# Conditioning vectors of a two-layer trunk: two empty steps between the last sum and the finishing products

## The chip, the cores and the metric

The kernel runs on one core of a Trainium2 chip. The metric is the device time of one execution in microseconds (us); of several executions the median is given. A profile is one execution, recorded by the hardware profiler; its span runs from the first to the last instruction. The engines are TensorE (PE, with its weight loads as PEld), VectorE (DVE), ScalarE (ACT), GpSimd (POOL) and SyncE (SP), whose queue issues nearly all transfers.

## The reference, cut to what matters

256 tokens of width 2048 go through two layers. Each layer has a token mixer (forgetting attention in layer 0, sliding-window attention in layer 1) and a gated feed-forward part with a short convolution. All is float32. What the change touches is the conditioning:

```python
c_act = jax.nn.silu(c)
for i in range(DEPTH):
    mod = c_act @ ada_w[i] + ada_b[i]
    sh1, sc1, g1, sh2, sc2, g2 = jnp.split(mod[:, None, :], 6, axis=-1)
    h = x * (1.0 + sc1) + sh1
    y = mixer(h)
    x = layer_norm(DEEPNORM_ALPHA * x + (1.0 + g1) * y, ...)
    h = x * (1.0 + sc2) + sh2
    y = conv_ffn(h, ...)
    x = layer_norm(DEEPNORM_ALPHA * x + (1.0 + g2) * y, ...)
```

Per layer six vectors of 2048 numbers are needed: shift and scale before the mixer (numbers 0 and 1), the gate behind it (2), and the same three for the feed-forward part (3, 4, 5). Each is a product of one row of 2048 with a 2048x2048 matrix, 16 MB that is read once.

## The kernel before, in words

Weights stream through SBUF in tiles of 128x1024 (512 KB). Every weight tile is split into a high part (`wh`, an ACT cast, L285) and a low part (`wl`, a DVE subtraction, L296), and PE multiplies both; one weight tile is twelve PE instructions of up to 512 columns in most stages. The function that PE runs for one weight tile, `go` in `stream`, ends with `tick`. The program thus advances tile by tile, and all side work is cut into steps that `tick` hands out.

Two of the twelve conditioning vectors are made in the opening; the other ten are made by the generator `ada_vector`, one after the other, in the order of `ada_list`: (0,2), (0,3), (0,4), (0,5), (1,0), (1,1), (1,3), (1,2), (1,4), (1,5), each a pair of layer and number. One vector is 32 sums: for each of 16 blocks of 128 rows, and for each half of the 2048 columns, a tile `wa` of the matrix (512 KB) is loaded by SP's queue (L434), and one DVE instruction adds it, scaled by a number per partition, to the accumulator `acc` (L438 for the first block, L440 for the others). What then stands in `acc` still has to be summed over its 128 partitions. That is done by finishing products on PE with a matrix of ones (`sm`): for a shift or a scale 16 products of one column each, four to a step; for a gate four products of 512 columns, one to a step. A last DVE instruction (`cv`, L463, or the gate's, L454) adds the bias.

How many steps `ada_vector` gets is set by a rate per weight tile, a number of the stage:

```python
    def ada_tick():
        ada["debt"] += ada["rate"]
        while ada["debt"] >= 1.0:
            ada["debt"] -= 1.0
            ada_step()
```

With the last step, which ends the vector, one vector takes 32 + 4 + 1 = 37 steps. The rate is 1.0 to 1.7 in layer 0's mixer, 0.52 and 0.8 in its feed-forward part, 0.3 at the very start of layer 1's mixer, then 0.95 and 0.9, and 0.4 in the last feed-forward part. When number 4 of a layer is done, the generator holds until the next boundary has been passed.

At a boundary between a mixer and a feed-forward part (or between layers) `between` calls `ada_need` for the shift and the scale that it needs. If one isn't done, `ada_need` hands out steps on the spot until it is. `modulate` follows: PE runs ten 512-column products (`warm`) that compute nothing that is used, transposes the first token block of `x`, runs six more, transposes the second block, and starts on the next weights, while DVE and ACT finish the normalisation.

The framework's scheduler puts the instructions on each engine in an order of its own, but those passed to `pin` with its second argument true keep the program's order among each other: the sums, the column products, `cv`, the residual of the last column block (L662 to L672) and the normalisation (L691) are among them. The loads are not. All `w`, `wa` and `ln` tiles share one pool of ten buffers that are taken in turn.

Of the kernel before, what the change touches and what calls it, by code (L numbers as in the profile page):

```python
# [41 lines left out]
def hybrid_trunk(ctx: ExitStack, tc: tile.TileContext, a: dict, out: bass.AP):  # L42
# [14 lines left out]
    def wtile(name="w"):  # L57
        return wp.tile([P, 2, WB], F32, tag="w", name=name)
# [7 lines left out]
    def bank(name="sm"):  # L66
        return psp.tile([P, 512], F32, tag="ps", name=name)
# [7 lines left out]
    def mm(o, lhsT, rhs, start=False, stop=False, **kw):  # L75
        return nc.tensor.matmul(o, lhsT, rhs, start=start, stop=stop, **kw)  # L76

    def pin(ins, on=True):

        if on:  # L80
            tc.keep_in_program_order(ins)
# [344 lines left out]
    def ada_vector(l, v):  # L426
        row = v % 3 == 2
        acc = cst.tile([P, D], F32, tag="acc", name="acc")
        part = lambda c, n: acc[:, c:c + n]
        step_ = D // 2  # L430
        for k in range(KC):
            for c in range(0, D, D // 2):
                w = wtile("wa").rearrange("p a f -> p (a f)")
                pin(nc.sync.dma_start(w, a["ada_w"][l, k * P:(k + 1) * P, v * D + c:v * D + c + D // 2]), False)  # L434
                for o in range(0, D // 2, step_):
                    ac, wo = part(c + o, step_), w[:, o:o + step_]
                    if k == 0:
                        pin(nc.vector.tensor_scalar_mul(ac, wo, cact[:, 0:1]), True)  # L438
                    else:
                        pin(nc.vector.scalar_tensor_tensor(ac, wo, cact[:, k:k + 1], ac,  # L440
                                                           op0=ALU.mult, op1=ALU.add), True)
                yield
        if row:
            while not ada["gate_free"]:
                yield
            ada["gate_free"] = False
            g = cst.tile([P, D], F32, tag="gate", name="gate")
            nc.gpsimd.dma_start(g, a["ada_b"][l, v * D:(v + 1) * D].partition_broadcast(P))
            for j in range(D // 512):
                ps = bank()  # L450
                mm(ps, ones, acc[:, j * 512:(j + 1) * 512], start=True, stop=True)
                yield
                gj = g[:, j * 512:(j + 1) * 512]
                nc.vector.scalar_tensor_tensor(gj, ps, 1.0, gj, op0=ALU.add, op1=ALU.add)  # L454
            gates[l, v] = g
            return
        ps = bank()
        for k in range(KC):
            pin(mm(ps[:, k:k + 1], part(k * P, P), ones[:, 0:1], start=True, stop=True))
            if k % 4 == 3:  # L460
                yield
        cv = cst.tile([P, KC], F32, tag=f"cv{v}", name="cv")
        pin(nc.vector.scalar_tensor_tensor(cv, ps[:, :KC], 1.0 if v % 3 else 0.0,  # L463
                                           acol[:, l, v * KC:(v + 1) * KC], op0=ALU.add, op1=ALU.add), True)
        cols[l, v] = cv
        if v == 4:
            ada["held"] = True

    def ada_step():
        if ada["gen"] is None:  # L470
            if not ada_list or ada.get("held"):
                return
            ada["gen"] = ada_vector(*ada_list.pop(0))
        if next(ada["gen"], ada) is ada:
            ada["gen"] = None
# [720 lines left out]
    for t in range(NT):  # L1196
        mu, rs, _ = moments[t]
# [34 lines left out]
```

## Time and profile before

| | |
|---|---|
| time, median of 3 runs | 2243.58 us (2242.21 to 2245.87) |
| the profiled execution: its time | 2244.19 us |
| its span | 2242.4 us |
| busy in the span: PE, DVE, ACT | 2201.2, 1854.7, 1193.0 us |
| moved by transfers | 602.68 MB |

The boundary before layer 0's feed-forward part shows in the trace at 461.75 us (the start of the ten warm products), the one before layer 1's mixer at 1213.75, and the one before layer 1's feed-forward part at 1491. Busy time of PE counts a product from its start to a modelled end, so that PE can be called busy while products come slower than they could; the idle time ahead of an instruction and the start times are the better guide.

### The profile page before, as it was taken

Reading aid. Unit: us, or ns where it says so; the run is one execution under the profiler, and the core shown is the slowest. Engines: PE = TensorE matmul, PEld = TensorE weight load, DVE = VectorE, ACT = ScalarE, POOL = GpSimd, SP = SyncE. Lnnn points to the kernel's source line nnn. Section 1 sums busy time; section 2 is a strip of 40 time slices with the busy share of each in tenths; the row PEclk is TensorE's granted clock in tenths of the full one; section 3 lists DMA queues with packets and bytes.
Section 4 is the critical chain, followed back from the end, with each engine's and each line's share of the span. In section 5 each row is a group of like instructions: output and inputs, shape, how many; then the busy total and the mean of one; then the engine's idle time right before and its main releaser. Section 6 shows DMA issues by size and latency. Waiting matters only on the chain.

```text
span 2242.4 us, 33367 instructions
## 1 busy us (share of the span) xinstructions
PE 2201.2 (98%) x12206; PEld 1890.4 (84%) x12206; DVE 1854.7 (83%) x2689; ACT 1193.0 (53%) x1873; POOL 20.0 (1%) x51
## 2 busy tenths in 40 slices
PE   7999999999999999999999999999999999999997
PEld 6999898788888888888888788888888888888886
DVE  7989998989988968978978989889988655676766
ACT  4546554455656433655534578646655533555542
POOL 0001000000000000000000000000000000000000
PEclk9999999999999999999999999999999999999999
DMA  9999999969878889878887867778887556666553
GB/s 359 390 358 336 358 364 334 336 217 313 304 240 282 320 290 330 284 230 282 281 307 281 283 194 266 235 248 291 284 270 239 185 195 190 189 190 193 189 196 114
DMA packets 287429, 602.68 MB, mean 269 GB/s; under 512 B 21846, under 2 KB 55576, under 8 KB 286752
## 3 DMA queue, kind: packets, MB, share of 16 engines
q1 hardware_dynamic: 286208, 595.86, 78.2%
q0 software_dynamic: 1056, 4.69, 0.7%
q8 instruction: 95, 1.56, 0.3%
q14 instruction: 70, 0.57, 0.1%
HBM read 598.37 MB, written 2.10 MB: 268 GB/s over the span
## 4 chain that ended last, share of the span: by engine, by line
PE 88%; DVE 7%; ACT 2%; issue 1%; DMA 1%; SPq 0%; DVEq 0%; ACTq 0%
PE wd L76 43%; PE xs L76 33%; PE ws L76 6%; DVE wl L296 2%; DVE acc L440 2%; PE sm L76 1%; PE S L76 1%; PE o L76 1%; ACT wh L285 1%; PE warm L76 1%; PE T L762 0%; DMA wo<-in_ada_w_dram 0%; DVE pr L738 0%; PE cps L76 0%; DVE oacc L590 0%
## 5 line engine op out<-in xcount | busy, mean ns | idle before, releaser
L285 ACT CAST wh<-w 128x1024 fp32r<-128x1024 f32 x728 | 764.3, 1051 | 775.9 <-PE wd L76 283.3
L296 DVE TENSOR_TENSOR wl<-w,wh 128x1024 fp32r<-128x1024 f32 x728 | 888.1, 1222 | 302.2 <-ACT wh L285 285.0
L76 PE MATMUL wd<-hHL,wh 128*128 128x512 f32 (+1 forms) x2832 | 718.2, 395 | 0.2
L76 PEld LDWEIGHTS wd<-hHL,wh 128*128 128x128 f32 x2832 | 504.6, 188 | 98.5 <-issue 2.9
L76 PEld LDWEIGHTS wd<-hHL,wl 128*128 128x128 f32 x2816 | 373.4, 188 | 31.0
L440 DVE SCALAR_TENSOR_TENSOR acc<-wa,cact,acc 128x1024 f32<-128x1024 f32 x300 | 380.9, 1279 | 0.1
L76 PE MATMUL wd<-hHL,wl 128*128 128x256 f32 x2816 | 380.0, 277 | 0.0
L76 PE MATMUL xs<-wh,gT 128*128 128x512 f32 x1408 | 350.0, 390 | 0.0
L76 PEld LDWEIGHTS xs<-wh,gT 128*128 128x128 f32 x1408 | 263.4, 188 | 54.2
L76 PE MATMUL xs<-wl,gT 128*128 128x512 f32 x704 | 189.6, 389 | 0.0
L76 PE MATMUL xs<-wh,hHL 128*128 128x512 f32 x704 | 185.5, 401 | 1.8 <-ACT wh L285 1.4
L76 PEld LDWEIGHTS xs<-wl,gT 128*128 128x128 f32 x704 | 132.1, 188 | 27.6
L76 PEld LDWEIGHTS xs<-wh,hHL 128*128 128x128 f32 x704 | 128.7, 190 | 28.6 <-ACT wh L285 1.6
L1119 ACT ACTIVATE u<-s,ccol 128x256 f32<-128x256 f32 x176 | 104.7, 599 | 68.3 <-DVE s L1114 49.6
L76 PE MATMUL ws<-hHL,wh 128*128 128x256 f32 x1024 | 132.6, 282 | 4.8 <-ACT wh L285 2.4
L76 PEld LDWEIGHTS ws<-hHL,wh 128*128 128x128 f32 x1024 | 124.8, 189 | 8.5 <-ACT wh L285 4.4
L76 PE MATMUL xs<-wh,oT 128*128 128x512 f32 x384 | 99.6, 397 | 1.7 <-ACT wh L285 1.6
L76 PE MATMUL xs<-wl,hHL 128*128 128x512 f32 x352 | 96.8, 395 | 0.8 <-DVE wl L296 0.6
L1120 DVE SCALAR_TENSOR_TENSOR u<-s,ccol,u 128x255 f32<-128x255 f32 x176 | 84.1, 479 | 5.7 <-ACT u L1119 5.7
L590 DVE SCALAR_TENSOR_TENSOR oacc<-wo,cact,oacc 128x512 f32<-128x512 f32 x111 | 79.5, 747 | 9.2 <-DMA wo<-in_ada_w_dram 5.3
L1122 DVE SCALAR_TENSOR_TENSOR u<-s,ccol,u 128x254 f32<-128x254 f32 x176 | 84.0, 478 | 1.1
L76 PEld LDWEIGHTS xs<-wh,oT 128*128 128x128 f32 x384 | 69.5, 188 | 16.6 <-ACT wh L285 2.8
(223 smaller groups left out, 1639.8 us busy)
## 6 DMA issues: line engine op xcount, KB each, us to landing
w<-in_ffn_w_up_dram SPq DMA_DIRECT2D x352, 512.0 KB, 4.6
wa<-in_ada_w_dram SPq DMA_DIRECT2D x320, 512.0 KB, 5.2
w<-in_ffn_w_down_dram SPq DMA_DIRECT2D x176, 512.0 KB, 4.3
w<-in_fox_w_in_dram SPq DMA_DIRECT2D x96, 512.0 KB, 6.6
wo<-in_ada_w_dram SPq DMA_DIRECT2D x128, 256.0 KB, 6.7
w<-in_swa_w_in_dram SPq DMA_DIRECT2D x40, 512.0 KB, 4.9
w<-in_fox_w_o_dram SPq DMA_DIRECT2D x32, 512.0 KB, 5.5
w<-in_swa_w_o_dram SPq DMA_DIRECT2D x32, 512.0 KB, 5.5
```

Source lines behind the costliest of these rows:

```text
L76: return nc.tensor.matmul(o, lhsT, rhs, start=start, stop=stop, **kw)
L285: pin(nc.scalar.copy(h, w), False)
L296: pin(nc.vector.tensor_tensor(l, w, f32(h), op=ALU.subtract), go in behind or tied[0] > 0)
L440: pin(nc.vector.scalar_tensor_tensor(ac, wo, cact[:, k:k + 1], ac, op0=ALU.mult, op1=ALU.add), True)
L590: nc.vector.scalar_tensor_tensor(ac, wk, cact[:, kc:kc + 1], ac, op0=ALU.mult, op1=ALU.add)
L1119: nc.scalar.activation(u, s, AF.Identity, bias=cw(CW, f), scale=cw(2, f))
L1120: nc.vector.scalar_tensor_tensor(u[:, 1:], s[:, :S - 1], cw(1, f), u[:, 1:], op0=ALU.mult, op1=ALU.add)
L1122: nc.vector.scalar_tensor_tensor(u[:, 2:], s[:, :S - 2], cw(0, f), u[:, 2:], op0=ALU.mult, op1=ALU.add)
```

## The change

Behind the last sum of a vector the generator now gives back the step twice without doing anything. Each vector so takes 39 steps in place of 37, and its finishing products are written two steps further down in the program. The rates, the products and the sums are the same.

```diff
@@ -440,6 +440,8 @@
                         pin(nc.vector.scalar_tensor_tensor(ac, wo, cact[:, k:k + 1], ac,
                                                            op0=ALU.mult, op1=ALU.add), True)
                 yield
+        for _ in range(2):
+            yield
         if row:
             while not ada["gate_free"]:
                 yield
```

Ten vectors times two steps make 20 steps, and each vector begins later than the one ahead of it by two more. Lines behind L442 have numbers that are higher by two in the changed kernel.

The first place is PE's order at the first vector, the gate (0,2), in layer 0's mixer. `sm<-acc,ones` is a finishing product, `ws` and `xs` are products of weight tiles, `T` is a transposition in the attention. Before:

```order
L76 MATMUL ws<-hHL,wh 128x256 x16
L76 MATMUL ws<-hHL,wl 128x256 x8
L76 MATMUL sm<-acc,ones 128x512
L762 MATMUL T<-ident,pr 128x128 x3
L76 MATMUL xs<-wh,hHL 128x512 x8
L76 MATMUL xs<-wl,hHL 128x512 x4
L76 MATMUL sm<-acc,ones 128x512 x2
```

and now:

```order
L76 MATMUL ws<-hHL,wh 128x256 x16
L76 MATMUL ws<-hHL,wl 128x256 x8
L764 MATMUL T<-ident,pr 128x128 x3
L76 MATMUL xs<-wh,hHL 128x512 x8
L76 MATMUL xs<-wl,hHL 128x512 x4
L76 MATMUL sm<-acc,ones 128x512
```

The first finishing product has moved behind one weight tile (eight and four products) and one set of transpositions.

The second place is PE's order at the boundary before layer 1's feed-forward part. Before, the 16 products of (1,4) stood in groups of four between the weight tiles of the output projection, the last group three weight tiles ahead of its end; the end itself read:

```order
L76 MATMUL xs<-wh,hHL 128x512 x4
L76 MATMUL xs<-wl,hHL 128x512 x2
L76 MATMUL warm<-ones 128x512 x10
L545 MATMUL sm<-ident,x 128x128 x4
L76 MATMUL warm<-ones 128x512 x6
L545 MATMUL sm<-ident,x 128x128 x4
```

Now:

```order
L76 MATMUL xs<-wh,hHL 128x512 x4
L76 MATMUL xs<-wl,hHL 128x512 x2
L76 MATMUL sm<-ones,acc 128x1 x16
L76 MATMUL warm<-ones 128x512 x10
L547 MATMUL sm<-ident,x 128x128 x4
L76 MATMUL warm<-ones 128x512 x6
L547 MATMUL sm<-ident,x 128x128 x4
```

All 16 products stand between the projection's last product and the first warm one: the vector isn't done when `between` asks for it, and `ada_need` hands out its last 11 steps there.

The third place is DVE's order at the same boundary, from the statistics of the second token block on. Before:

```order
L668 BN_AGGR mv<-stats 128x2
L670 TENSOR_SCALAR rs<-mv 128x1
L691 TENSOR_SCALAR x<-x,mv,rs 128x256 x2
L513 TENSOR_SCALAR t<-sm,G,B 128x256 x2
L516 TENSOR_TENSOR hHL<-t,hHL 128x256 x2
```

Now:

```order
L670 BN_AGGR mv<-stats 128x2
L672 TENSOR_SCALAR rs<-mv 128x1
L440 SCALAR_TENSOR_TENSOR acc<-wa,cact,acc 128x1024 x4
L465 SCALAR_TENSOR_TENSOR cv<-sm,acol 128x16
L725 TENSOR_TENSOR G<-cv,lcol 128x16
L726 TENSOR_TENSOR B<-cv,lcol 128x16
L727 TENSOR_TENSOR B<-B,cv 128x16
L693 TENSOR_SCALAR x<-x,mv,rs 128x256 x2
```

The last four sums, `cv` and the three instructions that use it now stand between the statistics and the normalisation; before, `cv` and the three stood ahead of the last residual. Six more sums of the vector now stand between the start of the third column block's residual and the last residual, where there was none.

## The prediction

> **What bounds the kernel now.** First the page's busy times, then the waits of PE alone, then the chain of waits.
>
> ```profile
> PE 2201.2 (98%) x12206; PEld 1890.4 (84%) x12206; DVE 1854.7 (83%) x2689; ACT 1193.0 (53%) x1873; POOL 20.0 (1%) x51
> PE 88%; DVE 7%; ACT 2%; issue 1%; DMA 1%; SPq 0%; DVEq 0%; ACTq 0%
> PE sm L76 <- DVE acc L440: 3.5, 2, 3.0
> PE xs L76 <- ACT wh L285: 3.0, 4, 1.4
> ```
>
> PE is the bound: it is idle for 2242.4 - 2201.2 = 41 us in all. So an edit that leaves PE's products alone can win only what PE waits for, and it loses whatever it puts ahead of PE's queue. In the third row finishing products (`sm`) wait for sums (L440) twice, 3.5 us together, 3.0 of them in one piece. That is the wait at which two steps' delay can be aimed. It is the first vector, (0,2):
>
> ```profile
> 254.79 1.10 PE L76 MATMUL ws<-hHL,wl 128*128 128x256 f32 x8
> 258.92 1.12 PE L76 MATMUL sm<-acc,ones 128*128 128x512 f32 x2 [3.02 <-DVE acc L440]
> 260.25 3.55 PE L76 MATMUL xs<-wh,hHL 128*128 128x512 f32 x8
> 257.58 2.48 DVE L440 SCALAR_TENSOR_TENSOR acc<-wa,cact,acc 128x1024 f32<-128x1024 f32 x2
> 256.00:259.00 3.00, 0.09 (x1) 0.09 (x1) 2.94 (x6) 3.00 (x9) 0.00 (x0) 1.00 1.01 387
> 259.00:262.00 3.00, 3.00 (x9) 2.18 (x10) 3.00 (x8) 2.74 (x7) 0.00 (x0) 0.67 1.06 408
> 262.00:264.00 2.00, 2.00 (x7) 1.52 (x7) 2.00 (x5) 1.71 (x5) 0.00 (x0) 0.65 1.04 388
> 264.00:266.00 2.00, 2.00 (x8) 1.15 (x7) 2.00 (x6) 2.00 (x7) 0.00 (x0) 1.00 0.99 367
> ```
>
> The last four rows are stretches of time with the busy time of each engine; the third number from the end is the granted PE clock. PE sits still for 3.02 us and then gets 0.67 and 0.65 of its clock for 5 us, which costs 3 x 0.33 + 2 x 0.35 = 1.7 us more. The stall is worth 4.7 us.
>
> **Part 1: the stall at (0,2) goes, -4.5.** In PE's new order a set of transpositions and one `xs` weight tile come ahead of the first product. A tile takes 2.75 us (from row to row below: 336.78 to 339.53), so with the transpositions some 3.1 us against 3.0 of waiting: the sum has just ended. PE gains up to 4.7 us here. Does it keep them?
>
> ```profile
> 285.00:350.00 65.00, 65.00 (x491) 61.67 (x490) 63.87 (x82) 34.90 (x64) 0.00 (x0) 1.00 0.98 359
> 336.78 1.99 PE L76 MATMUL xs<-wh,hHL 128*128 128x512 f32 x8
> 339.53 1.99 PE L76 MATMUL xs<-wh,hHL 128*128 128x512 f32 x8
> 341.35 1.08 PE L76 MATMUL xs<-wl,hHL 128*128 128x512 f32 x4
> 338.07 1.22 DVE L296 TENSOR_TENSOR wl<-w,wh 128x1024 fp32r<-128x1024 f32 x1
> ```
>
> From 285 to 350 DVE is busy for 63.87 of 65 us. At the end of it the low half that PE reads at 341.35 was finished at 338.07 + 1.22 = 339.29: PE has 2.06 us in hand, less than the 4.7. But DVE has less to do as well. At a fixed rate the two empty steps of (0,2) put off two sums up to there, 2 x 1.2 = 2.4 us of DVE. So 2.06 + 2.4 = 4.5 of the 4.7 can be kept.
>
> ```profile
> 350.00:375.00 25.00, 25.00 (x121) 20.94 (x120) 18.66 (x26) 8.16 (x14) 0.00 (x0) 1.00 0.92 346
> 375.00:437.00 62.00, 57.33 (x259) 44.25 (x258) 59.10 (x89) 28.95 (x48) 0.00 (x0) 1.00 0.92 329
> 437.00:461.00 24.00, 24.00 (x119) 20.23 (x118) 17.54 (x23) 7.70 (x8) 0.00 (x0) 1.00 0.78 267
> ```
>
> From 350 to 375 PE never waits and DVE has room, so the lead is carried on. From 375 to 437 DVE is busy for 59.10 of 62 us and PE is idle for 4.7; loads wait there for buffers that DVE frees. By then four sums (two vectors' empty steps) lie behind, and they come in the last weight tiles of the stretch, so that DVE's work inside it is about the same and the stretch is shifted as a whole. The four sums end where DVE has room (17.54 of 24 us). I keep -4.5. Bounds: 0 if DVE and the loads give all of it back, and -4.7 - 4.7 = -9.4 if DVE's four sums less also end PE's waiting from 375 to 437.
>
> In the other eight vectors nothing is gained: PE's waits for sums are these 3.5 us in all.
>
> **Part 2: sums that come later, 0.** A rate that is fixed and vectors that take 39 steps for 37 put sums off. In the feed-forward parts DVE's work is covered by PE, and sums there can move freely. In layer 1's mixer about as many sums fall into the first half as before. What was put off all along comes due at the end of its output projection: six sums more before its last residual, and four behind it.
>
> ```profile
> 1466.00:1476.00 10.00, 10.00 (x53) 8.54 (x52) 10.00 (x13) 3.16 (x3) 0.00 (x0) 1.00 1.04 397
> 1476.00:1488.40 12.40, 12.40 (x63) 10.44 (x63) 5.26 (x9) 3.15 (x3) 0.00 (x0) 1.00 0.70 240
> 365.82 2.48 DVE L440 SCALAR_TENSOR_TENSOR acc<-wa,cact,acc 128x1024 f32<-128x1024 f32 x2
> ```
>
> The last row gives the price: two sums in 2.48 us, with the small overlap of records 1.2 us each. Six are 7.2 us. In the 12.4 us up to 1488.4, where the last residual begins, DVE is idle for 7.1 and loses `cv` and its three followers (0.6) to a later place. It just fits; should it not, the residual starts late by a microsecond. I count 0, with 0 to +1.5 as bounds (the upper end also for attention steps of layer 1 that stand behind a sum more).
>
> **Part 3: the boundary before layer 1's feed-forward part, +10.5.** Rows of before there, PE first, then DVE:
>
> ```profile
> 1490.49 0.63 PE L76 MATMUL xs<-wl,hHL 128*128 128x512 f32 x2
> 1490.96 2.44 PE L76 MATMUL warm<-ones 128*128 128x512 f32 x10
> 1495.06 0.71 PE L545 MATMUL sm<-ident,x 128*128 128x128 f32 x4
> 1488.40 0.69 DVE L662 TENSOR_TENSOR t<-xs,gate 128x512 f32<-128x512 f32 x1 [1.35 <-PE xs L76]
> 1493.64 0.15 DVE L670 TENSOR_SCALAR rs<-mv 128x1 f32<-128x1 f32 x1
> 1494.54 0.74 DVE L691 TENSOR_SCALAR x<-x,mv,rs 128x256 f32<-128x256 f32 x2 [0.75 <-POOL rs L673]
> ```
>
> PE went on to the warm products at 1490.96, and from there to the second block's transpositions at 1495.06 it had 4.1 us of queued work that hid the normalisation. Now 16 finishing products stand ahead of the warm ones, and they need sums that DVE starts only after L670, at 1493.7. Four sums end at 1493.7 + 4 x 1.2 = 1498.5, the third at 1497.3. The loads aren't late: each takes the buffer of the tile ten loads earlier, which by DVE's order is freed between the residual of the third block and 1483, and a load lands in 5.2 us (below), so by 1489. The products:
>
> ```profile
> 342.43 1.92 PE L76 MATMUL sm<-ones,acc 128*128 128x1 f32 x16
> 10.58 1.83 PE L76 MATMUL cps<-cact,wo 128*128 128x1 f32 x8 [7.03 <-DMA wo<-in_ada_w_dram]
> 14.95 2.48 PE L76 MATMUL warm<-ones 128*128 128x512 f32 x5
> wa<-in_ada_w_dram SPq DMA_DIRECT2D x320, 512.0 KB, 5.2
> ```
>
> In the midst of work 16 take 1.92 us (0.12 each). Behind 7.03 us of idleness eight take 1.83 (0.23 each), and five warm products 2.48 (0.5 each, against 2.44 for ten above). Here PE will have been idle from 1491.1 to 1497.3, 6.2 us, so the slow price applies.
>
> At full clock: eight products beside the fourth sum, eight from 1498.5 to 1499.5. The warm ones start there and not at 1490.96: +8.5, the lower end. With the slow clock: 16 x 0.23 = 3.7 us from 1497.3 to 1501.0, +10.0. After (0,2)'s stall the low clock lasted 5 us from the first product; here that is until 1502.3, so 1.3 us of warm products go at half pace, +0.65. That gives +10.7; +11.5 as upper end if the clock comes back a microsecond or two later. `cv`, its followers (0.6) and the normalisation (0.74) then run under the warm products, and 4.1 us behind their start the transpositions follow as before. Whatever comes later on PE is PE-bound, with nothing that could take the delay up. I take +10.5.
>
> The skill's rule on this: the Trainium skill ("TensorE: Matmul & The Clock Gate", Part 1) has PE drop to half rate after at least one idle window of about 3.4 us, and recover after about as long of sustained work. By that, (0,2)'s 3.0 us wouldn't have cost the clock, and the boundary would lose half of 3.4 us, an estimate of 1.7: the sum would be -3.0 + 8.5 + 1.7 = +7.2. The trace shows 0.67 after 3.02 us, so the row decides for (0,2).
>
> **The sum.** -4.5 + 0 + 10.5 = +6.0, on the profiled execution's own 2244.19: 2250.2. That execution lies 0.6 above the median of the runs shown, 2243.58, so as a median 2249.6; I say 2250.
>
> **Rivals.**
>
> *The wait moves, and nothing is won in layer 0.* DVE is nearly full from 285 to 350 and PE has only 2 us in hand at its end. If the two sums put off don't fall where I have them, or the loads (0.98 of the DMA share there) are the bound and not DVE, the 4.7 us come back as waits of `xs` products. Against it: the sums put off are 512 KB loads put off as well. Price: 0 + 10.7 = +10.7, 2254.
>
> *DVE is relieved and the kernel is not slower.* In 375 to 437 PE waits for what DVE and its buffers hold up:
>
> ```profile
> PE xs L76 <- DVE wl L296: 1.2, 3, 0.5
> PE sm L76 <- DVE acc L440: 0.5, 1, 0.5
> ```
>
> These rows, with the 3.0 us for `wh` above, are all of PE's waits from 350 to 440, 4.7 us. If four sums less ahead of it (4.8 us of DVE, 2 MB of loads) end them, layer 0 gives -9.4, and with the boundary at its lower end of +8.5 the kernel comes out at -0.9, 2243. It decides where DVE reaches 375 more than 4 us earlier relative to PE. Against it: PE comes earlier as well, and the same 20 or so sums lie within that stretch.
>
> *The change doesn't do what it says at the boundary*: the scheduler's order stands, but the four sums are ready sooner because DVE reaches the residual's end early. It can't: that end follows PE's last product by 2.5 us (1491.1 to 1493.7). With half of it saved the cost would be +7 and the sum +2.5, 2246.
>
> **How the numbers follow.** My forecast, +3 to +9: 0.57. Nothing won in layer 0 (+9 to +12.5): 0.18. Layer 0 wins much more, or the boundary costs less (-1 to +3): 0.20. Below that, with both: 0.05. The range from 2244.5 (+1) to 2256 (+12.5) leaves out less than 2 in 10. 0.2% of the time is 4.5 us, about what a measurement tells from no change. A quarter of the forecast's chance lies under +4.5. So slower: 0.43 + 0.18 = 0.61, rounded to 0.62; same 0.34; faster 0.04.
>
> **What would show it.** At (0,2) no idle time ahead of the first `sm`, and the clock at 1.00 around it. The warm products at the boundary before layer 0's feed-forward part, in the chain of waits of before
>
> ```profile
> 461.75 2.27 PE warm L76 x10
> ```
>
> start earlier by 4 to 5 us. At the third boundary an idle PE of 6 us with DVE's sums named as releaser, a granted clock well under 1 in the 5 us behind it, and the time from the projection's last product to the second transpositions up from 4.6 to about 15 us. The distances from one boundary to the next otherwise as before, within a microsecond or two. I am wrong if the first boundary comes no earlier (the wait moved), if it comes 8 us earlier (DVE was the bound), or if PE at the third boundary is idle for 3 us or less.

## The result, and the profile after

The changed kernel takes 2254.51 us (median of 6 runs, 2253.34 to 2257.42). The kernel before took 2244.6 beside it (median of 6 runs, 2242.21 to 2246.53). The ratio is 1.0049, interval 1.0039 to 1.0059: the change costs about 10 us. 2250 was predicted, with a range from 2244.5 to 2256 and "slower" as the likeliest sign. The sign and the places are right, but +6.0 was worked out and +9.9 was measured, and the sum hides larger errors of both signs.

The page of the changed kernel has these rows:

```profile
span 2252.7 us, 33379 instructions
PE 2203.3 (98%) x12206; PEld 1891.6 (84%) x12206; DVE 1854.4 (82%) x2689; ACT 1192.9 (53%) x1873; POOL 20.9 (1%) x51
PE 80%; DVE 10%; DMA 5%; ACT 2%; issue 2%; SPq 0%; DVEq 0%; ACTq 0%
```

The span is 10.3 us longer. PE's busy time grew by only 2.1 us, so 8.2 us of the loss are PE sitting idle. In the chain of waits PE's share went from 88% to 80%, to the benefit of DVE and DMA. The DMA part is no loss: those loads stand on the chain in the first 133 us, and at 240 us PE is at the same product in both kernels to within 0.1 us. The chain says more when the three boundaries are compared. Its rows give the start, the length and the work; the ten `warm` products mark each boundary. After:

```profile
455.95 2.27 PE warm L76 x10
1207.88 2.27 PE warm L76 x10
1498.41 4.48 PE warm L76 x10
```

and before:

```profile
461.75 2.27 PE warm L76 x10
1213.75 2.27 PE warm L76 x10
1491.12 2.27 PE warm L76 x10
```

The first boundary comes 5.8 us earlier, the second 5.9 us earlier, the third 7.3 us later, and there the ten products take 4.48 us and not 2.27 (the chain counts them from the end of what released them, the timeline below from their start). All the gain is made in layer 0's mixer, and nearly all the loss at the third boundary.

**The gain.** PE's timeline at the first vector, after:

```profile
256.73 2.09 PE L76 MATMUL xs<-wh,hHL 128*128 128x512 f32 x8
258.66 1.08 PE L76 MATMUL xs<-wl,hHL 128*128 128x512 f32 x4
259.58 1.02 PE L76 MATMUL sm<-acc,ones 128*128 128x512 f32 x2
```

No idle time stands ahead of `sm` (before: 3.02 us), since a weight tile runs in its place. The busy times of the engines by stretch (PE, PEld, DVE, ACT, POOL, then the granted PE clock, the DMA share and GB/s), after:

```profile
256.00:259.00 3.00, 2.79 (x13) 2.21 (x14) 2.93 (x6) 3.00 (x10) 0.00 (x0) 1.00 1.02 365
259.00:262.00 3.00, 2.94 (x14) 1.84 (x13) 3.00 (x8) 2.75 (x7) 0.00 (x0) 1.00 0.99 360
375.00:437.00 62.00, 59.57 (x267) 46.86 (x266) 58.89 (x86) 29.74 (x46) 0.00 (x0) 1.00 0.92 325
1467.00:1482.55 15.55, 15.21 (x67) 12.21 (x65) 15.55 (x17) 5.28 (x5) 0.00 (x0) 1.00 0.99 373
1482.30:1491.40 9.10, 0.00 (x0) 0.00 (x0) 8.83 (x16) 4.17 (x6) 2.59 (x3) 0.71 1.01 373
1491.40:1498.20 6.80, 6.78 (x32) 6.78 (x32) 1.16 (x1) 0.00 (x0) 0.00 (x0) 0.50 0.76 295
1486.04:1503.11 17.07, 11.69 (x45) 10.62 (x46) 7.68 (x14) 4.04 (x6) 2.04 (x2) 0.50 0.61 229
```

In the first two rows the clock stays at 1.00 where it had been 0.67. In the third, PE is busy for 59.57 of 62 us (before: 57.33): from 375 to 437 it waits 2.2 us less. Between 240 and 470 PE's waits were 3.5, 3.0 and 1.2 us before. Above 0.3 us this one alone is left:

```profile
PE xs L76 <- DVE wl L296: 2.9, 5, 1.1
```

That is some 4.5 us of waiting less; with the 1.7 us of the low clock it makes 6.2, of which 5.8 show at the first boundary.

**The loss.** The timeline of the third boundary, after. The bracket behind a row is the idle time ahead of it and what ended that:

```profile
1481.59 0.62 PE L76 MATMUL xs<-wl,hHL 128*128 128x512 f32 x2
1482.55 0.69 DVE L664 TENSOR_TENSOR t<-xs,gate 128x512 f32<-128x512 f32 x1
1487.63 0.15 DVE L672 TENSOR_SCALAR rs<-mv 128x1 f32<-128x1 f32 x1
1487.70 4.86 DVE L440 SCALAR_TENSOR_TENSOR acc<-wa,cact,acc 128x1024 f32<-128x1024 f32 x4
1491.42 6.99 PE L76 MATMUL sm<-ones,acc 128*128 128x1 f32 x32 [9.21 <-DVE acc L440]
1498.27 4.61 PE L76 MATMUL warm<-ones 128*128 128x512 f32 x10
1502.68 0.81 PE L547 MATMUL sm<-ident,x 128*128 128x128 f32 x4
1505.65 0.74 PE L76 MATMUL wd<-hHL,wh 128*128 128x256 f32 x4
```

Before, the same first weight product of the feed-forward part stood here:

```profile
1496.08 0.65 PE L76 MATMUL wd<-hHL,wh 128*128 128x256 f32 x4
```

From the start of the last `xs` to the first `wd` it was 1496.08 - 1490.49 = 5.6 us and is now 1505.65 - 1481.59 = 24.1, so 18.5 more. The rows add up: 9.2 of waiting, 1498.27 - 1491.42 = 6.9 of finishing products, and 1502.68 - 1498.27 = 4.4 in place of 2.3 for the ten `warm`, together 18.2; the other 0.3 lie in the small distances between these rows. Not all of it is loss, since the 16 products stood in the projection before. The view by stretch, limited to instructions on `acc`, has their cost there (PE first, in 32 records), before:

```profile
1437.00:1491.10 54.10, 3.79 (x32) 4.19 (x32) 13.18 (x11) 1.00 0.84 291
```

So 3.8 of the 18.5 only moved, and the boundary costs 14.7. With -5.8 at the first boundary, -0.1 in layer 0's feed-forward part, +0.8 in layer 1's mixer (its last `xs` starts 8.9 earlier; 5.9 of these it brought along and 3.8 are the moved products) and +0.7 behind the boundary, the sum is +10.3, the difference of the spans.

### The profile page after: what moved, and what is told of

It is laid out like the page before. It is cut to its first block, busy times and chain, and to the rows that moved or that the text cites. A ratio compares the mean times of both kernels' runs of the same rounds, so it can differ in the third digit from the quotient of the medians.

```text
span 2252.7 us, 33379 instructions
## 1 busy us (share of the span) xinstructions
PE 2203.3 (98%) x12206; PEld 1891.6 (84%) x12206; DVE 1854.4 (82%) x2689; ACT 1192.9 (53%) x1873; POOL 20.9 (1%) x51
## 4 chain that ended last, share of the span: by engine, by line
PE 80%; DVE 10%; DMA 5%; ACT 2%; issue 2%; SPq 0%; DVEq 0%; ACTq 0%
PE wd L76 43%; PE xs L76 29%; DMA wo<-in_ada_w_dram 4%; PE ws L76 4%; DVE acc L440 3%; DVE wl L296 3%; PE sm L76 1%; DMA w<-in_fox_w_in_dram 1%; ACT wh L285 1%; PE o L76 1%; PE S L76 1%; PE warm L76 1%; DVE pr L740 1%; ACT pr L752 0%; ACT pr L744 0%
```

## The experiments

The theory after the result: the two empty steps win 4 to 6 us in layer 0's mixer and lose some 15 at the third boundary; the two have nothing to do with each other but that the steps are counted together. The rivals: the gain is only the first vector's stall; the loss there is only the clock, or only the waiting for late sums; or the steps cost something everywhere. Each edit is against the changed kernel. "Before" is timed beside each.

### Only the first vector delayed

```diff
-        for _ in range(2):
+        for _ in range(2 if (l, v) == (0, 2) else 0):
```

> The two empty steps only in the first vector (0,2). Theory (the wait of 3.0 us and the low clock behind it are the main part of the mixer's gain): -4 us, 2240 to 2241 us, and no idle time ahead of its first finishing product. Rival (the gain in the mixer comes from DVE, which has sums put off by all three vectors' steps): -2 us or less, since only two of the sums are put off, with PE's waits for low halves in 375 to 437 us as before. The clock-blind rival would be -3.0 us.

Measured: 2242.29 us against 2243.42, ratio 0.9995 (0.9986 to 1.0004): no difference that can be told. The gain expected for the first vector alone did not come. In the profiled execution, the third longest of the eleven (2244.36 us), the first boundary stands at 461.83 in the chain, where it stood before. PE's waits and then its timeline at the *next* vector, (0,3), say why for this execution:

```profile
PE sm L76 <- DVE acc L440: 1.2, 1, 1.2
```

```profile
344.34 1.92 PE L76 MATMUL sm<-ones,acc 128*128 128x1 f32 x16 [1.24 <-DVE acc L440]
```

The sums of (0,3) begin two steps later but its finishing products are not put off, so the wait appears there. Its stretches:

```profile
344.30:346.10 1.80, 1.76 (x16) 1.79 (x17) 1.80 (x2) 0.00 (x0) 0.00 (x0) 1.00 0.95 345
347.04:350.45 3.41, 3.41 (x10) 2.65 (x9) 1.76 (x2) 1.05 (x1) 0.00 (x0) 0.50 1.03 399
439.20:442.61 3.41, 3.41 (x9) 2.63 (x9) 3.41 (x5) 0.02 (x1) 0.00 (x0) 0.50 1.02 377
```

Behind 1.2 us of waiting and 1.8 us of one-column products the clock is 0.50 for 3.41 us, which costs 1.7 us more. At (0,4), behind one-column products again, it falls a second time, for another 1.7. In this execution the first rival of the prediction holds (the wait moves and nothing is won), but only for one vector alone, and perhaps not in every execution: the eleven spread from 2238.80 to 2245.03 us, and their mean clock is 0.998 in the four shortest and 0.996 in three of the four longest.

### Only the three vectors of layer 0's mixer delayed

```diff
-        for _ in range(2):
+        for _ in range(2 if (l, v) in ((0, 2), (0, 3), (0, 4)) else 0):
```

> The two empty steps only in the three vectors of layer 0's mixer. Theory (two separate effects: about -5.8 us in layer 0's mixer, and about +16 us from the catch-up at the boundary before layer 1's feed-forward part): no catch-up there, so the first effect alone, 6 us faster than before, about 2239 us, and the ten warm products of the first boundary at about 456 us as in the changed kernel. Rival (the mixer's gain is given back later, at the same boundary, because DVE and the loads are the bound): within 2 us of before, 2243 to 2246.

Measured: 2238.02 us against 2243.42, -5.4; ratio 0.9979 (0.9970 to 0.9988). Its chain:

```profile
455.63 2.27 PE warm L76 x10
1484.98 2.27 PE warm L76 x10
```

The first boundary is 6.1 us earlier than before and the third is too: the lead is carried through a whole layer without loss, and the third boundary's ten products run at full clock. This version is faster than both kernels.

### All vectors but those three delayed

```diff
-        for _ in range(2):
+        for _ in range(0 if (l, v) in ((0, 2), (0, 3), (0, 4)) else 2):
```

> The two empty steps in the seven vectors from (0,5) on, none in layer 0's mixer. Theory: the first boundary at 461.7 us as before, the catch-up of 11 steps as in the changed kernel, so 15 to 16 us slower than before, about 2260 us. Rival (part of the loss comes from layer 0's mixer, whose sums end later): about as slow as the whole change, 2254 us, with less than 11 us lost.

Measured: 2260.30 us against 2243.42, +16.9; ratio 1.0073 (1.0060 to 1.0086). Its chain:

```profile
462.32 2.27 PE warm L76 x10
1504.97 4.47 PE warm L76 x10
```

The two halves add up to -5.4 + 16.9 = +11.5, against +9.9 for the whole change: separate to within 2 us.

### Delayed in the first two vectors, and one step in place of two

Three more kernels ask how much of the delay the gain needs. Two steps in (0,2) and (0,3):

```diff
-        for _ in range(2):
+        for _ in range(2 if (l, v) in ((0, 2), (0, 3)) else 0):
```

> The two empty steps in (0,2) and (0,3) only. Theory (with (0,2) alone the wait moved on to (0,3), 1.2 us and the low clock behind it, and two steps there end that chain): 4 to 5 us faster than before, 2239 to 2240 us; what is left to the three vectors' 5.4 us is (0,4)'s small wait. Rival (each vector passes the wait on to the next): no more than 1 to 2 us faster, with PE waiting for a sum at (0,4), 430 to 440 us.

Measured: 2239.18 us against 2244.06, -4.9; ratio 0.9981 (0.9973 to 0.9990). With the second vector put off as well, nearly all of the gain is there.

One step in the mixer's three vectors:

```diff
-        for _ in range(2):
+        for _ in range(1 if (l, v) in ((0, 2), (0, 3), (0, 4)) else 0):
```

> One empty step in place of two, in the three vectors of layer 0's mixer only. Theory (the wait to be covered is 3.0 us and one step there is about one weight tile; with one step in all vectors the first boundary came 5.2 us earlier): 4.5 to 5.5 us faster than before, 2238.5 to 2239.5 us. Rival (the second step carries a good part): 2 to 3 us faster at most.

Measured: 2239.18 us against 2244.21, -5.0; ratio 0.9979 (0.9970 to 0.9988). The second step adds nothing to the time that can be told. In the trace no idle time stands ahead of (0,2)'s first finishing product any more; a wait of 1.5 us for ACT, which the kernels with two steps don't have, has come up behind these products.

One step in all ten vectors:

```diff
-        for _ in range(2):
+        for _ in range(1):
```

> One empty step per vector in place of two. The boundary before layer 1's feed-forward part then catches up 5 steps: the 16 finishing products and the last DVE instruction, no sums. Theory (the loss there is mostly the wait for the four sums, and behind it the halved clock): PE goes on to the products without a wait, they stand there in place of elsewhere, and only the clock can be lost (2 to 4 us); layer 0's mixer gains 4 to 6 us; together 2239 to 2243 us. Rival (a catch-up of any size at that place costs most of what the change loses, since everything behind it waits for the vector): 2248 us or more.

Measured: 2241.67 us against 2244.06, -2.4; ratio 0.9992 (0.9983 to 1.0001). The interval reaches past 1, so this one is at most slightly faster. Of the gain of 5 us about half is lost. At the third boundary 5 steps are left in place of 11, and none of them is a sum: only the 16 products and `cv` are caught up. The timeline of its third boundary, and behind it the stretches (columns as above), tell most of the clock:

```profile
1482.39 3.63 PE L76 MATMUL sm<-ones,acc 128*128 128x1 f32 x32
1485.88 3.96 PE L76 MATMUL warm<-ones 128*128 128x512 f32 x10
```

```profile
1483.25:1486.66 3.41, 3.41 (x28) 3.28 (x29) 3.24 (x8) 1.60 (x3) 1.13 (x2) 1.00 1.04 416
1486.66:1490.07 3.41, 3.41 (x11) 2.65 (x10) 1.46 (x8) 1.63 (x3) 0.56 (x1) 0.50 0.91 354
```

PE is busy in all of these 6.8 us. Yet behind 3.5 us of one-column products, 0.8 us into the `warm` ones, the clock falls to 0.50 for 3.41 us, and ten `warm` take 3.96 us. The ones that were there to keep the clock up come too late.

### Faster steps in the feed-forward part, so that nothing is left to catch up

```diff
-            then(lambda: ada.update(rate=(0.52, 0.4)[l]))
+            then(lambda: ada.update(rate=(0.57, 0.4)[l]))
...
-                ada["rate"] = (0.8, 0.4)[l]
+                ada["rate"] = (0.86, 0.4)[l]
```

> The whole change, with the rates of layer 0's feed-forward part raised from 0.52 and 0.8 to 0.57 and 0.86, so that ten sums fall there that the change puts off, and nothing is caught up at the boundary. Theory (the two empty steps themselves cost nothing in the seven later vectors): as with the two steps in the mixer alone, 2237 to 2240 us. Rival (more sums in the feed-forward part are not covered by PE there): 2241 us or more, with PE waiting for low halves between the first two boundaries.

Measured: 2240.69 us against 2244.06, -3.4; ratio 0.9983 (0.9975 to 0.9992), the top of what was expected and a little over. All twenty empty steps are kept, and the loss is gone all the same. So the empty steps themselves cost little; what costs is that the vector isn't done when it is asked for. By the medians 2 us less are won than with the mixer's vectors alone, but the two intervals overlap. PE's waits in layer 1's mixer (1207 to 1490) of this kernel would account for it:

```profile
PE qp L1064 <- DVE qq L1056: 3.1, 4, 1.7
PE sm L76 <- DVE acc L440: 1.1, 1, 1.1
```

Before, the first of these was 2.2 us and the second didn't stand there: together +2.0. Whether these waits come from the higher rates or from the empty steps in layer 1 these runs don't tell.

### Warm products in the wait for the sums

Is the loss the waiting, or the clock behind it? Here 40 products that compute nothing are put ahead of the catch-up, which fills PE's idle time:

```diff
         ada_need(l, v)
+        if (l, v + 1) not in cols:
+            warm(40)
         ada_need(l, v + 1)
```

> The whole change, with 40 more warm products (40 x 0.231 = 9.2 us of PE work that computes nothing used) ahead of the 16 finishing products at the boundary before layer 1's feed-forward part, where PE is idle for 9.2 us in the changed kernel. Theory (the idle wait halves the clock, and the finishing products and the ten warm ones then run at half pace for 11 us): the sums end as before, the 32 recorded products take 3.8 us and not 6.9, the ten warm ones 2.3 and not 4.5, so about 5 us faster than the change, 2249 us. Rival (the finishing products are slow there for another reason, as waiting for DVE or loads): the time of the change, 2254.5 us, or slower if the 40 products reach past the sums.

Measured: 2252.57 us against 2243.42, +9.2; ratio 1.0040 (1.0027 to 1.0052). Expected were 3.5 us less. Its timeline, and behind it the stretches:

```profile
1483.46 9.23 PE L76 MATMUL warm<-ones 128*128 128x512 f32 x40
1492.83 4.86 PE L76 MATMUL sm<-ones,acc 128*128 128x1 f32 x32
1497.54 4.61 PE L76 MATMUL warm<-ones 128*128 128x512 f32 x10
```

```profile
1491.78:1495.19 3.41, 3.27 (x26) 2.77 (x25) 2.19 (x2) 0.00 (x0) 0.00 (x0) 1.00 0.83 288
1495.19:1502.02 6.83, 6.83 (x24) 5.76 (x24) 1.26 (x6) 0.00 (x0) 0.00 (x0) 0.50 0.48 181
```

The idle time is filled, and the clock is at 1.00 when the finishing products begin. It falls 2.4 us into them. They take 4.86 us in place of 6.99, 2.1 less, but the ten `warm` behind them are as slow as ever. So the waiting isn't needed for the low clock: it comes with narrow products behind full work too. The boundary gets shorter by the 2.1 us, but 1.4 of them are lost ahead of it (its last `xs` starts at 1482.99, not 1481.59). They are lost in layer 0's mixer, where the two programs are the same: the first boundary stands at 457.42 and not at 455.95. The finishing products of (0,4) and the stretch behind them, first in this kernel and then in the changed one:

```profile
441.97 1.84 PE L76 MATMUL sm<-ones,acc 128*128 128x1 f32 x16
443.88:447.29 3.41, 3.41 (x9) 2.63 (x9) 2.13 (x2) 0.01 (x1) 0.00 (x0) 0.50 1.00 359
442.11 1.84 PE L76 MATMUL sm<-ones,acc 128*128 128x1 f32 x16
443.88:447.29 3.41, 3.41 (x20) 2.93 (x19) 2.28 (x3) 1.05 (x1) 0.00 (x0) 1.00 1.01 361
```

The same products in the same order cost the clock in one execution and not in the other, 1.7 us. So the 1.4 us aren't due to the 40 products, and falls like this one are part of what separates single executions.

### Two warm products behind each four of the catch-up as well

```diff
             if k % 4 == 3:
+                if ada.get("late"):
+                    warm(2)
                 yield
...
+        if (l, v + 1) not in cols:
+            warm(40)
+            ada["late"] = True
         ada_need(l, v + 1)
+        ada["late"] = False
```

> As with the 40 warm products ahead of the caught-up ones, and two more warm products behind each four of these (8 x 0.231 = 1.85 us of added PE work). Theory (one-column products count as idle for PE's clock: it was at 1.00 when they began and fell to 0.50 before their end): the clock stays above 0.9, the 32 recorded products take about 3.8 us and the ten warm ones behind them 2.3, so 3.2 us less than with the 40 alone, less the 1.85 added: 1 to 1.5 us faster than that, 2251 us. Rival (the clock falls from something else, as the end of the 40 products itself): half clock as before, and 1.85 us slower than with the 40, 2254 us.

Measured: 2252.84 us against 2244.06, +8.8; ratio 1.0043 (1.0030 to 1.0056). The clock should have held and didn't: two are too few. The stretch at the low clock in this kernel, which begins at the second of the four groups and ends behind the last `warm`:

```profile
1494.41:1504.65 10.24, 10.24 (x35) 8.68 (x34) 1.26 (x6) 0.00 (x0) 0.00 (x0) 0.50 0.29 114
```

### Eight of them, with one step in place of two

The same switch with `warm(8)`, without the 40, and on the kernel with one empty step, where there is no wait for sums:

```diff
-        for _ in range(2):
+        for _ in range(1):
...
             if k % 4 == 3:
+                if ada.get("late"):
+                    warm(8)
                 yield
```

> One empty step per vector, and at the caught-up boundary eight warm products (1.85 us) behind each four finishing products (eight records, 0.95 us). Theory (one-column products count as idle for the clock, and it needs a larger share of full products than the two per four that did not hold it): the clock stays at 1.00 and the last group of 18 warm products takes 4.2 us, 0.231 each; the added 32 products cost 7.4 us and the held clock gives 2 back, so 5 us slower than the one-step kernel without them, 2247 us. Rival (it falls from the gap in the projection's work, whatever runs there): half clock at the end of the groups, 2249 us or more.

Measured: 2247.85 us against 2244.21, +3.6; ratio 1.0018 (1.0009 to 1.0027). The end of its catch-up in the timeline, and its four groups as one stretch:

```profile
1491.42 0.95 PE L76 MATMUL sm<-ones,acc 128*128 128x1 f32 x8
1492.23 4.35 PE L76 MATMUL warm<-ones 128*128 128x512 f32 x18
```

```profile
1483.21:1492.23 9.02, 9.02 (x57) 8.00 (x56) 4.26 (x10) 4.01 (x6) 1.70 (x3) 1.00 0.75 300
```

The clock stays at 1.00, and 18 `warm` take 4.35 us (0.24 each, against 0.40 in the kernel with one step and none between). So mixing does hold the clock. It doesn't pay: 32 more products at 2.27 / 10 us are 7.3 us, and win back 3.96 - 2.27 = 1.7 us for the ten at the end.

## Why the prediction was right or wrong

**What bounds the kernel: right.** Time went and came mainly where PE waits or its clock falls.

**Part 1, -4.5 at (0,2): right in kind, -5.8 measured.** The stall and its clock are gone, as forecast. The lead was kept, and 2.2 us of waiting between 375 and 437 went as well, which the part had as its lower bound ("end PE's waiting") and counted at nothing. The -5.8 is one trace; the first boundary of the four other kernels with the same delay in this mixer stands between 455.57 and 457.42, 4.3 to 6.2 us earlier than before. The upper bound, that the wait moves, is what the trace of one vector alone shows (-1.1 us in the median, no difference that can be told). What the part didn't see is what holds the gain: that the next vector's finishing products are put off as well (-4.9 with the first two).

**Part 2, "It just fits" and 0: wrong.** The step counted six sums, 7.2 us less 0.6, into DVE's 7.1 idle us before the last residual. But those idle microseconds belonged to a projection that still held the 16 products. Without them it is 3.8 us shorter, DVE's room is 7.1 - 3.8 = 3.3, and 3.3 of the 6.6 don't fit. The trace has DVE busy for 15.55 of 15.55 us up to the residual at 1482.55. This now begins 0.96 us behind the start of the last `xs`, where it began 2.09 ahead of it: 3.0 late, outside the bounds of 0 to 1.5. PE's wait is 9.2 us for that reason and not 6.2.

**Part 3, +10.5: its mechanism right, three terms mis-sized and one left out, 14.4 measured (14.7 with the small distances between the rows).** With the projection's moved time set against it:

| term | predicted | measured |
|---|---|---|
| PE idle before the third sum's products | 6.2 | 9.2 |
| the products, up to the first `warm` | 3.7 | 6.9 |
| ten `warm` at a low clock | +0.65 | +2.1 |
| the same products no longer in the projection | 0 | -3.8 |
| sum | 10.5 | 14.4 |

The products: "16 take 1.92 us" took the count of the trace's row for a count of products. The order has 16 where the trace has 32, so a product of this form is two records, and the row shows half as many. At full clock 16 are 3.8 us (the row of `acc` above), at 0.50 they are 6.9. The step chose the slow price and came out at the fast one.

The clock: "the low clock lasted 5 us from the first product" carried a length from a place where 512-column products follow a stall to one where one-column products do. In the changed kernel the clock fell in the midst of the wait and was 0.50 from 1486.04 to 1503.11. It came back 4.8 us behind the first 512-column product; at (0,2) that was 4.5 (258.92 to 263.41). The narrow products in between did nothing for it, so that the ten `warm` ran at half pace from first to last. The prediction set a rule of the Trainium skill ("TensorE: Matmul & The Clock Gate", Part 1) against (0,2): half rate after an idle window of about 3.4 us, back after about as long of sustained work. The traces agree with the length (the clock is low for 3.41 us or a multiple of it, see the last section), but not with a window that has to be idle throughout: of the 3.41 us ahead of the fall at (0,2) PE was busy for 1.08, and the kernel with one step shows a fall with no idle time at all. The rule's recovery after sustained work does agree, if 512-column products alone count as such.

The term left out: part 3 priced what came to the boundary and not what left the projection. It hid half of the other errors, so that the sum came out as near as it did is in part luck.

**The rivals.** "The wait moves, and nothing is won in layer 0" forecast 2254, near the measured time, and is false all the same: the first boundary came 5.8 us earlier. "DVE is relieved" has a part in -5.8 but not the -9.4 that it needs. "The sums are ready sooner" is refuted by the 9.2 us of waiting.

**What stays open.** How many 512-column products among narrow ones hold the clock: two behind each four (eight records) don't, eight do. What the 0.7 us behind the boundary are. That the two halves give +11.5 and the whole +9.9 lies within their intervals (2 to 3 us to each side for each half) and needs no cause.

## What to carry to other kernels

When a background job is put off by a fixed count, find the place where its result is asked for and count the steps that are left there: what was free in the gaps of other work is paid in full at the deadline, with the clock on top. An edit that helps in one stage is given to that stage alone (the mixer's vectors alone: 2238.02 us, 5.4 under before), or the rate is raised so that the deadline holds. When work leaves a stretch, count again how much room that stretch has, for every engine.

## What the runs showed of the hardware

The clock of PE is 1.00 or 0.50 in these traces; the values in between are means over a stretch in which it changed. Cut where it changes, the rows at (0,2) in the kernel before read:

```profile
256.59:260.00 3.41, 1.08 (x4) 0.56 (x5) 3.35 (x5) 3.41 (x8) 0.00 (x0) 1.00 1.03 409
260.00:263.41 3.41, 3.41 (x12) 2.73 (x11) 3.41 (x9) 3.03 (x9) 0.00 (x0) 0.50 1.03 395
```

Apart from the end of each trace, the clock is low for 3.41 us or a multiple of it: 3.41 here, at (0,3) and (0,4) and with one step, 6.83 with the 40 `warm` products, 10.24 with two between, 17.07 in the changed kernel. The two falls in the kernel with the first vector alone, at 347.04 and 439.20, lie 27 times 3.413 us apart. This looks as if the clock were set once in every 3.41 us by what PE did in them, at points that fall differently in each execution. That would explain (0,4), where the same products cost the clock in one execution and not in another; no run here moves these points by itself.

A PE that is busy need not keep its clock. In the kernel with one step the 3.41 us ahead of the fall held 2.6 us of one-column products, 0.8 of 512-column ones and no idle time. Groups of 0.8 us of one-column and 1.9 us of 512-column products left the clock at 1.00 (eight `warm` between). After a fall the clock came back only behind 512-column products: 4.2 us after the first of them began in the kernel with one step, 4.5 with the 40 `warm` and at (0,2) before, 4.8 in the changed kernel.

An f32 product of one column, as used here, leaves two records, 0.12 us each at full clock and 0.22 at 0.50.
